# Softmax times V: the last head's scores in parts of 2, 2, 2, 1, 1 rows, with a store moved behind the first part

## Chip, cores, metric

The kernel runs on one core of a Trainium2 chip. The metric is the device time of that core in microseconds (us). A profile has its own zero, so moments of two profiles are compared with each other only to some tenths of a us, and where it matters against a landing of data in the same profile.

## The reference, cut to what matters

```
scores: 8 x 12 x 1024 x 1024, v: 8 x 12 x 1024 x 64, float32
attn = exp(scores - max);  attn = attn / (sum(attn) + 1e-8);  out = attn @ v
```

There are 96 heads of 4 MB of scores each, which are read once. The kernel leaves the maximum out and gets the sum from a column of ones beside V.

## The kernel before

Heads are worked on in groups of four; a loop runs over the 24 groups. A head is 128 partitions with 8 rows each. For each row ScalarE (ACT) makes the exponentials (two rows at a time), TensorE (PE) transposes them in 8 pieces into PSUM, VectorE (DVE) copies the transposed row to SBUF, and TensorE multiplies it with V in 8 matmuls of 65 columns. After four or eight rows VectorE divides by the sums. All loads and stores are issued by one engine (SP) into one queue.

```python
def finish(u):                        # the second product of one row
    ...
    for c in range(C):                # C = 8
        nc.tensor.matmul(
            out=bank[:, g * M : (g + 1) * M],          # M = 65
            lhsT=pt[:, c * P : (c + 1) * P],
            rhs=st["vones"][:, c, 0:M],
            start=(c == 0), stop=(c == C - 1),
        )
    ...
def load_next(k, n0):                 # heads 0 and 1 of the next group
    if k < AHEAD - 2:
        load(k, (n0 + (AHEAD + k)) % BH, cond=n0 < BH - AHEAD)

def last(n0):                         # at the end of a group
    with tc.If(n0 < BH - 2 * AHEAD) as cmp:            # the ordinary groups
        ...
    with cmp.Else():
        with tc.If(n0 < BH - AHEAD) as cmp2:           # the last group but one
            ...
            load(AHEAD - 2, BH - 2, (4, 4))            # the last head but one, in two parts
            load(AHEAD - 1, BH - 1, (4,))              # the last head: four rows,
            store(n0, AHEAD - T)                       # a store of two heads (512 KB),
            load(AHEAD - 1, BH - 1, (2, 1, 1), 4)      # and the other four rows
        ...
```

For each row TensorE issues, in its queue, the row's transposes, then the second product of an earlier row.

The softmax here doesn't subtract the row's maximum and nothing guards it: scores larger than these inputs give would overflow.

## Time and profile before

| | before |
|---|---|
| time, first three runs | 1066.0 us median (1065.59 to 1067.29) |
| busy: PE / DVE / ACT | 68% / 73% / 70% of the span |
| DMA | full in 39 of 40 slices, 434 GB/s |
| last row of scores landed, in the profile | 1052.8 us |
| VectorE's last multiply of the output by the reciprocal sums ended | 1059.4 us |
| span of the profile | 1063.5 us |

How to read it: the queue is full to the end, so the time is the bytes at the queue's rate, plus a tail of about 11 us behind the last bytes. Timeline: start, length, engine, line, operation; in brackets the idle time before and what ended it.

```profile
1049.29 0.69 DVE L285 COPY pt<-psT 128x1024 f16<-128x1024 f16 x1 [0.27 <-PE L146]
1050.25 0.69 DVE L285 COPY pt<-psT 128x1024 f16<-128x1024 f16 x1 [0.27 <-PE psO L146]
```

These are rows 0 and 1 of the last head. The copies start 0.96 us apart, though one takes 0.69, and each time a completion of TensorE ends 0.27 us of idle time. Row 1 had been ready in ScalarE long before.

### The profile page before, as it was taken

The page shows a single profiled execution, that of the slowest core. Times are in us where ns is not written, and L with a number is a line of the kernel's source. Part 1 is how long each engine was busy: PE and PEld are TensorE (multiplying, and loading weights), DVE is VectorE, ACT ScalarE, POOL GpSimd, SP SyncE. Part 2 cuts the span into 40 slices and gives each one's busy share as a digit, 9 for nine tenths or more (in the row PEclk, how much of TensorE's full clock was granted, in tenths as well). Part 3 has the DMA queues.
Part 4 walks back from the last instruction along what each step waited for, and adds up shares of the span by engine and source line. Part 5 has one row for each costly group of instructions (what it writes and reads, how often), then busy time and mean ns, then how long its engine had stood idle before and what let it go on. Part 6 is the DMA issues. An engine that isn't in the chain of part 4 may idle for free. (4 is left out here: it accounts for less than half of the span.)

```text
span 1063.5 us, 32373 instructions
## 1 busy us (share of the span) xinstructions
PE 725.8 (68%) x12288; PEld 669.1 (63%) x12288; DVE 780.7 (73%) x1589; ACT 743.2 (70%) x480; POOL 48.1 (5%) x31
## 2 busy tenths in 40 slices
PE   2487766667776767677676666767766767766676
PEld 2476666566666666566575666756666666666575
DVE  3488767777677776777777777777678776777777
ACT  3767776676766758676676766777766767667586
POOL 0000000000000000000000000000000000000000
PEclk9789888988879888988888888898889898888989
DMA  9999999999999999999999999999999999999995
GB/s 394 433 420 436 422 434 433 433 435 433 434 433 434 424 438 433 429 428 433 435 427 439 434 433 434 427 436 425 434 429 434 434 434 434 434 431 425 439 426 242
DMA packets 24915, 453.05 MB, mean 426 GB/s; under 512 B 2768, under 2 KB 2768, under 8 KB 9296
## 3 DMA queue, kind: packets, MB, share of 16 engines
q1 hardware_dynamic: 24912, 453.00, 99.2%
q8 instruction: 3, 0.05, 0.0%
HBM read 436.21 MB, written 25.17 MB: 434 GB/s over the span
## 5 line engine op out<-in xcount | busy, mean ns | idle before, releaser
L265 ACT ACTIVATE p_nat<-s_nat 128x2048 f16<-128x2048 f32 (+1 forms) x408 | 705.2, 1800 | 308.9 <-DMA s_nat<-in_scores_dram 218.0
L279 PE MATMUL psT<-order,p_nat 128*128 128x128 f16 x6144 | 556.7, 243 | 231.2 <-ACT p_nat L265 224.7
L285 DVE COPY pt<-psT 128x1024 f16<-128x1024 f16 x768 | 513.7, 687 | 221.8 <-PE L146 94.1
L279 PEld LDWEIGHTS <-p_nat 128*128 128x128 f16 x6144 | 437.8, 122 | 255.2 <-ACT p_nat L265 252.5
L146 PEld LDWEIGHTS <-pt 128*128 128x128 f16 x6144 | 296.9, 107 | 133.6 <-DVE pt L285 128.1
L146 PE MATMUL psO<-vones,pt 128*128 128x65 f16 x3072 | 183.6, 203 | 58.5 <-DVE pt L285 56.6
L146 PE MATMUL psO_whole<-vones,pt 128*128 128x65 f16 x3072 | 186.1, 209 | 42.6 <-DVE pt L285 42.6
L212 DVE COPY vones<-v_half 32x512 f16<-32x512 f16 x384 | 109.2, 284 | 28.3 <-POOL v_half L208 17.0
L208 POOL CAST v_half<-v_sb 128x2048 f16<-128x2048 f32 x25 | 47.4, 1894 | 995.4 <-DMA v_sb<-in_v_dram 915.9
L130 DVE TENSOR_TENSOR out_sb<-psO,recip 64x256 f32<-64x256 f32 x192 | 81.1, 423 | 6.1
L130 DVE TENSOR_TENSOR out_sb<-psO_whole,recip 64x512 f32<-64x512 f32 x96 | 66.1, 688 | 3.0
L258 ACT ACT_TABLE_LOAD x24 | 30.8, 1283 | 1.8 <-ACTq L309 1.4
L125 DVE RECIPROCAL recip<-psO 128x4 f32<-128x4 f32 x96 | 17.1, 179 | 18.4 <-PE psO L146 17.2
L258 ACT ACTIVATE spare<-order 128x1 f16<-128x1 f16 x48 | 9.5, 198 | 0.3
L125 DVE RECIPROCAL recip<-psO_whole 128x8 f32<-128x8 f32 x48 | 9.5, 197 | 0.0
L71 DVE MEMSET vones<- 128x16 f16 x4 | 0.2, 72 | 0.8 <-PEq L326 0.8
L62 DVE CAST order<-ident 128x128 f16<-128x128 f32 x1 | 0.2, 226 | 0.4 <-POOL ident masks.py:199 0.4
masks.py:199 POOL TENSOR_SCALAR_AFFINE_SELECT ident<-ident 128x128 f32<-128x128 f32 x1 | 0.3, 292 | 0.1
masks.py:197 POOL MEMSET ident<- 128x128 f32 x1 | 0.2, 204 | 0.3 <-POOLq L326 0.3
L326 POOL MEMSET const-float32-0.0<- 128x1 f32 x1 | 0.1, 98 | 0.2 <-issue 0.2
L326 POOL MEMSET const-bfloat16-1.0<- 128x1 bf16 x1 | 0.1, 101 | 0.0
L326 POOL MEMSET const-uint8-127<- 128x1 uint8 x1 | 0.1, 101 | 0.0
(1 smaller groups left out, 0.1 us busy)
## 6 DMA issues: line engine op xcount, KB each, us to landing
s_nat<-in_scores_dram SPq DMA_DIRECT2D x96, 4096.0 KB, 34.1
v_sb<-in_v_dram SPq DMA_DIRECT2D x24, 1024.0 KB, 35.7
out_dram<-out_sb SPq DMA_DIRECT2D x47, 512.0 KB, 25.3
s_nat<-in_scores_dram SPq DMA_DIRECT2D x3, 2048.0 KB, 32.7
s_nat<-in_scores_dram SPq DMA_DIRECT2D x1, 1024.0 KB, 25.6
s_nat<-in_scores_dram SPq DMA_DIRECT2D x2, 512.0 KB
out_dram<-out_sb SPq DMA_DIRECT2D x2, 256.0 KB, 2.1
```

The costliest lines, as they stand in the source:

```text
L62: nc.vector.tensor_copy(out=order16[:].rearrange("p (t j) -> p t j", t=T), in_=ident32[:].rearrange("p (j t) -> p t j", t=T),)
L71: nc.vector.memset(vo[:, :, D : D + 2], 1.0)
L125: nc.vector.reciprocal(out=recip, in_=psO[:, :, :, D : D + 1])
L130: nc.vector.tensor_tensor(out=rows.rearrange("j (b g) d -> j b g d", g=G), in0=psO[part, :, :, 0:D], in1=recip[part].to_broadcast([W, last ...
L146: nc.tensor.matmul(out=bank[:, g * M : (g + 1) * M], lhsT=pt[:, c * P : (c + 1) * P], rhs=st["vones"][:, c, 0:M], start=(c == 0), stop=(c ...
L208: nc.gpsimd.tensor_copy(out=v_half[:], in_=v_sb[:])
L212: copy = nc.vector.tensor_copy(out=vones_bufs[k][s * Q : (s + 1) * Q, :, 0:D].rearrange("i (h l) d -> i h l d", l=L), in_=v_half[k * Q : ( ...
L258: table = nc.scalar.activation(out=spare[:], in_=order16[:, 0:1], func=EXP)
L265: exp = nc.scalar.activation(out=p_nat[:, g : g + rows, :].rearrange("p r (x v) -> p x r v", v=Q * L), in_=s_bufs[k][:, r + g : r + g + ro ...
L279: nc.tensor.transpose(out=psT[:, c * P : (c + 1) * P], in_=p_row[:, c // L, c % L, :], identity=order16[:],)
L285: copy = nc.vector.tensor_copy(out=pt[:], in_=psT[:])
L326: nc = _bacc.Bacc("TRN2", target_bir_lowering=False, num_devices=1)
```

## The change

Its intent: ScalarE waits 1.02 us for the four-row part of the last head. With two rows first, and the store only then, it can go on at once.

```diff
                 load(AHEAD - 2, BH - 2, (4, 4))
-                load(AHEAD - 1, BH - 1, (4,))
+                load(AHEAD - 1, BH - 1, (2,))
                 store(n0, AHEAD - T)
-                load(AHEAD - 1, BH - 1, (2, 1, 1), 4)
+                load(AHEAD - 1, BH - 1, (2, 2, 1, 1), 2)
```

## The prediction

> **What bounds the kernel now.** I read the page's slices first, then the list of who waited for whom, then the timelines of the DMA queue's issuing engine (SP), ScalarE and VectorE over the last 60 us.
>
> ```profile
> DMA  9999999999999999999999999999999999999995
> GB/s 394 433 420 436 422 434 433 433 435 433 434 433 434 424 438 433 429 428 433 435 427 439 434 433 434 427 436 425 434 429 434 434 434 434 434 431 425 439 426 242
> ```
>
> The DMA engines are full in 39 of 40 slices, at about 434 GB/s; ACT (70%), DVE (73%) and PE (68%) have slack. So the length is the bytes over this rate (453 MB / 434 GB/s = 1044 us) plus what is left to compute after the last bytes. The changed code moves the same bytes, so only two things can move: whether the queue ever runs dry, and the tail behind the last loads. The tail starts from when each load was put in the queue; SP's timeline from 1005 us:
>
> ```profile
> 1006.69 0.36 SPq L166 DMA_DIRECT2D out_dram<-out_sb  x1
> 1007.68 6.48 SPq L189 DMA_DIRECT2D s_nat<-in_scores_dram  x3
> 1024.19 0.35 SPq L166 DMA_DIRECT2D out_dram<-out_sb  x1
> 1024.72 28.28 SPq L189 DMA_DIRECT2D s_nat<-in_scores_dram  x5
> 1053.29 6.71 SPq L166 DMA_DIRECT2D out_dram<-out_sb  x3
> ```
>
> The third load of the second line (issued 1013.83) is the last head's four-row part; the store at 1024.19 is the one behind it, then come two rows (1024.72), one row (1025.26), one row (1030.62). The last two L189 entries are the switched-off loads of the final iteration. Issue to landing, from the DMA view cut to one issue at a time: four rows 32.7 us, store 23.7, two rows 25.6. So they land at 1046.5, 1047.9 and 1050.3. For the two single rows the view has no landing, but the two switched-off loads wait on the same semaphores and went at 1051.70 and 1052.91, so they landed just before, about 1051.6 and 1052.8. The spacing is 1.2 us per 512 KB in the queue, whether load or store.
>
> ScalarE, where the last head begins:
>
> ```profile
> 1041.77 3.72 ACT L265 ACTIVATE p_nat<-s_nat 128x2048 f16<-128x2048 f32 x2 [0.19 <-PE L279]
> 1045.39 0.19 ACT L258 ACTIVATE spare<-order 128x1 f16<-128x1 f16 x1
> 1046.61 7.65 ACT L265 ACTIVATE p_nat<-s_nat 128x2048 f16<-128x2048 f32 x5 [1.02 <-DMA s_nat<-in_scores_dram]
> ```
>
> It is done with the head before at 1045.6, idles 1.02 us for the four-row part, and then runs its five exponentials (2, 2, 2, 1, 1 rows) without a gap over 0.1 us to 1054.26. Starts, from narrower windows: 1046.61, 1048.42, 1050.45, 1052.27, 1053.2. The third starts just after its landing at 1050.3: it is bound by data as much as by ScalarE.
>
> VectorE to the end:
>
> ```profile
> 1050.85 0.20 DVE L125 RECIPROCAL recip<-psO_whole 128x8 f32<-128x8 f32 x1
> 1051.27 0.69 DVE L285 COPY pt<-psT 128x1024 f16<-128x1024 f16 x1 [0.21 <-PE L279]
> 1051.99 1.41 DVE L130 TENSOR_TENSOR out_sb<-psO_whole,recip 64x512 f32<-64x512 f32 x2
> 1053.43 1.89 DVE L285 COPY pt<-psT 128x1024 f16<-128x1024 f16 x3
> 1055.23 0.17 DVE L125 RECIPROCAL recip<-psO 128x4 f32<-128x4 f32 x1
> 1055.32 0.66 DVE L285 COPY pt<-psT 128x1024 f16<-128x1024 f16 x1
> 1056.01 0.88 DVE L130 TENSOR_TENSOR out_sb<-psO,recip 64x256 f32<-64x256 f32 x2
> 1056.92 0.69 DVE L285 COPY pt<-psT 128x1024 f16<-128x1024 f16 x1
> 1058.33 0.18 DVE L125 RECIPROCAL recip<-psO 128x4 f32<-128x4 f32 x1 [0.72 <-PE psO L146]
> 1058.55 0.87 DVE L130 TENSOR_TENSOR out_sb<-psO,recip 64x256 f32<-64x256 f32 x2
> ```
>
> This carries the end. From the copy at 1051.27 VectorE is never idle until the last copy ends at 1057.61. In program order that first copy is row 2 of the last head (third of eight), then come the normalisation of the head before (1.41), the copies of rows 3, 4, 5, a reciprocal, row 6, half a normalisation, and row 7. The last copy is not waiting for ScalarE, which ended at 1054.26: it stands in VectorE's own line, and the line's start is set by row 2. Row 2 hangs on the second exponential (1048.42 to 1050.33), its transposes (from 1050.38) and the copy at 1051.27.
>
> **What the Trainium skill says.** "DMA: Bandwidth & Descriptors", section "Queues, rings and completion order": descriptors are consumed in ring order on each DMA engine. The trace agrees: the landings above come in the order of issue, at the queue's rate. The section "Why a DMA increments its semaphore by 16 and not by 1" says that only the full count of 16 means that all data landed, so a part is usable when its slowest engine is through; the DMA share falls well under full from 1049 on while rows still land to 1052.8, which agrees. The section "Anatomy of one DMA — SWDGE (gpsimd) path" has a fixed 2.0 us per DMA (for the GpSimd path), and says that DMA engines do not wait on semaphores, the issuing sequencer does. In this full queue the fixed part does not show (1.2 us for a whole 512 KB part); it shows on the last, lone stores of 256 KB (2.1 us). So a fifth part is nearly free.
>
> **The change part by part.** (1) First part two rows instead of four: 1 MB less in front of the store. From the spacing, 2 x 1.2 = 2.4 us: rows 0 and 1 land at 1046.5 - 2.4 = 1044.1, before ScalarE is free at 1045.6. The first exponential starts at about 1045.6, which takes away the whole wait of 1.02. (2) The store follows: 1044.1 + 1.4 = 1045.5 (the store's own step was 1047.9 - 1046.5). (3) The new two-row part, rows 2 and 3, is now behind the store: 1045.5 + 2.4 = 1047.9. Adding the 0.1 us seen from landing to start (1046.5 to 1046.61), the second exponential starts at 1048.03 where it was 1048.42: 0.39 sooner, with a new wait of about 0.6 for DMA in front of it. (4) Rows 4 and 5, 6, 7 have the same bytes ahead of them as before: 1050.3, 1051.6, 1052.8. Exponentials three to five start as before, ScalarE ends at 1054.2 as before. (5) One more DMA in the kernel: its completion on a full queue, I take 0.0 to 0.05 us.
>
> On VectorE: row 2's copy moves from 1051.27 to 1050.88. The line behind it (1.41 + three copies at 0.6 + 0.1 + 0.66 + 0.88 + 0.69) moves as a block if no member waits. Row 4: its exponential ends at 1052.36, transposes take 0.64, ready about 1053.1; its new place is 1053.65. Row 5 follows at 1054.25, ready about 1053.7. Row 6: exponential ends 1053.31, transposed about 1054.0, place 1054.9. Row 7: exponential ends 1054.26, transposed by about 1055.3, place 1056.5. None is short, so the block keeps the 0.39 us. The last stores go 0.39 sooner. Sum of the tail: -0.39 + 0.03 = about -0.4 us.
>
> (6) The hidden part. The instruction order shows that the DMA semaphores, eight, are used in rotation, and that branches of unequal DMA count are evened out by register steps and waits. The extra DMA makes SP in the ordinary branch (the iterations before the last two) wait also for the landing of the store of heads 0 and 1, before the next iteration's first load. Before, it already waits there for the load of head 1:
>
> ```profile
> SPq L231 <- SPq L231: 134.2, 21, 7.1
> ```
>
> In the iteration at 979 that wait ended at 986.8, and the next load was issued at 988.19. The store follows head 1's load in the queue, so its landing is 1.2 to 1.4 us later, and the load would be issued at about 989.6. But that load's data is used at 1020.98, 32.8 us after issue, while its own 4.19 MB need 4.19 / 434 = 9.7 us. So some 23 us of transfers stand ahead of it, and 1.4 us less of lead costs nothing. The next load waits for ScalarE (issued 994.31), and isn't touched. In the last-but-one iteration the last row's load must now wait for that store's landing, about 1032, twenty microseconds before its turn. No cost.
>
> Total: 1066.0 - 0.4 = 1065.6 us.
>
> **The rivals.** All of ScalarE's 1.02 us comes off the end: 1065.0. For it speaks that this is the only wait for data in the tail, and the intent is plainly this; against it that rows 2 and 3 are put behind the store, and rows 4 to 7 land no sooner. Nothing comes off: 1066.0; so it is if ScalarE's last three exponentials, whose data do not move, set the end. Against it is VectorE's unbroken line of 6.3 us that starts at row 2. The wait for the store in (6) starves the queue: at 1.4 us in 22 iterations it would be +31 us, 1097, slower by 2.9%; the 23 us of lead speak against it. A short dip from smaller parts (8 KB a row of partition instead of 16) would cost under 0.5 us: the two-row part before the change kept the pace of 1.2 per 512 KB.
>
> **Range and chances.** The effect is under 0.1%, less than the spread of the three runs before (1065.59 to 1067.29). The range is that spread around 1065.6, a bit widened for another chip: 1064.2 to 1067.0. Faster by over 2% would need 21 us, and the tail behind the last data is only about 11 us long: 0.003. Slower needs the starved queue: 0.007. The same: 0.99.
>
> **What would show it.** The first exponential of the last head at about 1045.6 with no wait; a new wait of about 0.6 for DMA before the second; the third to fifth at the same places; VectorE's block and its last multiply about 0.4 sooner; SP's wait at L231 longer by about 1.3 us in each iteration, with DMA still full in 39 slices. I am wrong if VectorE's line breaks at row 4 (then the gain is 0 to 0.2), if the part behind the store lands later than 1048, or if the slices show DMA under 9 before the last.

## The result

| | before | changed |
|---|---|---|
| times | 1065.8 us median of 4 (1065.54 to 1067.29) | 1066.18 us median of 4 (1065.52 to 1066.19) |
| ratio | | 0.9999, 95% interval 0.9982 to 1.0017: the same |
| span of the profile | 1063.5 | 1063.6 |

A ratio here is the mean time of one kernel's fast runs over that of the other's of the same rounds, so not quite the ratio of the medians.

The slices of the changed kernel: DMA is full up to the last, as before.

```profile
DMA  9999999999999999999999999999999999999995
```

ScalarE at the last head, in the changed kernel:

```profile
1045.29 1.90 ACT L265 ACTIVATE p_nat<-s_nat 128x2048 f16<-128x2048 f32 x1
1047.88 1.92 ACT L265 ACTIVATE p_nat<-s_nat 128x2048 f16<-128x2048 f32 x1 [0.70 <-PE psT L279]
1050.30 3.81 ACT L265 ACTIVATE p_nat<-s_nat 128x2048 f16<-128x2048 f32 x3 [0.50 <-PE psO L146]
```

The wait of 1.02 is gone. A wait of 0.70 stands before the second exponential instead, and one of 0.50 before the third. The profile names PE as what ended them; but rows 2 and 3 landed at 1047.8 (issue at 1023.22 plus 24.6 us) and the exponential started 0.1 later, so it was the load. The second exponential is 0.54 us sooner than before (1048.42), the later ones 0.15, which is as much as the data landed sooner in this profile.

VectorE to the end, in the changed kernel:

```profile
1049.38 0.69 DVE L285 COPY pt<-psT 128x1024 f16<-128x1024 f16 x1 [0.27 <-PE psT L279]
1050.34 0.69 DVE L285 COPY pt<-psT 128x1024 f16<-128x1024 f16 x1 [0.27 <-PE L279]
...
1051.36 0.69 DVE L285 COPY pt<-psT 128x1024 f16<-128x1024 f16 x1 [0.21 <-PE L146]
1052.08 1.41 DVE L130 TENSOR_TENSOR out_sb<-psO_whole,recip 64x512 f32<-64x512 f32 x2
...
1058.64 0.88 DVE L130 TENSOR_TENSOR out_sb<-psO,recip 64x256 f32<-64x256 f32 x2
```

Nothing moved forward here: the copies and the last multiply are 0.09 us *later* than before. The data came sooner, the exponentials came sooner, and VectorE did not notice. The copies of rows 0 and 1 are again 0.96 us apart with 0.27 of idle time each.

Last, SP's own wait where the groups' branches meet; the columns are us in all, times, longest:

```profile
SPq L231 <- SPq L231: 161.4, 43, 7.2
```

It was 134.2 before: (161.4 - 134.2) / 22 = 1.24 us more in each ordinary iteration, for the landing of the store. The queue stayed full, so it cost nothing.

### The profile page after: what moved, and what is told of

Its sections match the earlier page's. It is cut to its first block, busy times and chain, and to the rows that moved or that the text cites. A ratio compares the mean times of both kernels' runs of the same rounds, so it can differ in the third digit from the quotient of the medians.

```text
span 1063.6 us, 32424 instructions
## 1 busy us (share of the span) xinstructions
PE 724.6 (68%) x12288; PEld 667.7 (63%) x12288; DVE 780.9 (73%) x1589; ACT 743.3 (70%) x480; POOL 48.0 (5%) x31
```

## The theory and its rivals

A semaphore is a counter by which one engine tells another how far it is. In the trace, every weight load and every matmul of TensorE adds one to one semaphore, 12288 of each. Of the steps between these additions in the kernel before, 22647 of 24578 are 30 ns; the two shortest are 29 ns. An extract of their times from the kernel before:

```
1050.013  1050.043  1050.073  1050.103  1050.133  1050.163  1050.193 ...
333 additions from 1046.9 to 1056.9 us; the kernel's only pause over 0.1 us
between 1043 and 1056.9 is one of 0.11 us at 1046.75
```

A row has 16 weight loads and 16 matmuls, so 32 x 30 ns = 0.96 us, exactly the spacing of the copies. TensorE itself is faster: earlier in the kernel before, at full clock, the transposes of successive rows start at 1028.35, 1029.05 and 1029.75, 0.70 us apart.

```profile
1028.35 0.61 PE L279 MATMUL psT<-order,p_nat 128*128 128x128 f16 x8
1029.05 0.61 PE L279 MATMUL psT<-order,p_nat 128*128 128x128 f16 x8
```

So TensorE's work gets ahead of its own count, and VectorE, which waits for the count, learns of a row late. Read from the traces (the ends of matmuls are modelled by the profile):

| last head | last transpose ended | its addition came | VectorE's copy started |
|---|---|---|---|
| before, row 1 | 1049.91 | 1050.22 | 1050.25 |
| before, row 2 | 1051.02 | 1051.24 | 1051.27 |
| changed, row 1 | 1049.52 | 1050.32 | 1050.34 |
| changed, row 2 | 1050.85 | 1051.34 | 1051.36 |

Each copy follows its addition by 0.02 to 0.03 us, and the addition follows the work by up to 0.80 us. In the changed kernel the transposes of row 2 also began late, at 1050.21: in TensorE's queue they stand behind a matmul that waits for VectorE's copy of row 0 (1049.38 to 1050.07), and that copy had itself waited for the count.

*Theory of the count:* the count, not the data, sets when row 2's copy starts, so the change has nothing to gain. *Rivals:* (a) the prediction's own, in which row 2's exponential sets it; (b) the landings of the last head; (c) the time of TensorE itself, in its array or in loading weights; (d) VectorE's own work; (e) TensorE's granted clock, which from 1034 to 1038 us was 0.60 in the changed kernel's profile and 1.00 in that of the kernel before.

Ten more kernels were run, two of them twice. The quantities to compare, all read from the traces: the *lag* is from the end of the second exponential (rows 2 and 3) to row 2's copy; the *tail* is from the landing of the last row to the end of VectorE's last multiply; the clock is TensorE's mean granted clock from 1034 to 1038 us. (One of them, split_fine, ended so much later that it does not stand in the table.)

| kernel | counts per row, last head | row 2's exponential ends | row 2's copy | lag | tail | clock | span |
|---|---|---|---|---|---|---|---|
| before | 32 | 1050.33 | 1051.27 | 0.94 | 6.64 | 1.00 | 1063.5 |
| changed | 32 | 1049.80 | 1051.36 | 1.56 | 6.87 | 0.60 | 1063.6 |
| cut_only | 32 | 1048.84 | 1051.73 | 2.89 | 7.42 | 0.74 | 1064.0 |
| narrow_after | 32 | 1050.41 | 1051.69 | 1.29 | 6.58 | 1.00 | 1063.9 |
| more_after | 48 | 1050.34 | 1052.25 | 1.91 | 10.19 | 1.00 | 1067.5 |
| half_before | 24 | 1049.96 | 1050.72 | 0.76 | 6.29 | 1.00 | 1062.9 |
| half_before2 | 24 | 1049.98 | 1050.74 | 0.76 | 6.29 | 1.00 | 1062.8 |
| half_after | 24 | 1049.12 | 1049.88 | 0.76 | 5.85 | 1.00 | 1062.1 |
| half_after2 | 24 | 1049.22 | 1050.53 | 1.31 | 6.42 | 0.80 | 1062.6 |
| half_cut | 24 | 1048.46 | 1049.74 | 1.29 | 5.69 | 1.00 | 1061.8 |
| split_before | 32 | 1051.93 | 1052.87 | 0.94 | 6.62 | 1.00 | 1065.0 |
| split_after | 32 | 1051.51 | 1052.27 | 0.76 | 6.27 | 1.00 | 1064.6 |
| split_late | 32 | 1050.49 | 1052.72 | 2.24 | 6.76 | 1.00 | 1065.1 |

## The experiments

### cut_only: the cut without the store's move

```diff
-                load(AHEAD - 1, BH - 1, (4,))
+                load(AHEAD - 1, BH - 1, (2, 2))
                 store(n0, AHEAD - T)
```

> The kernel before with the last head in 2,2,2,1,1 rows, but the store left where it was, behind row 3 (one half of the change alone). Theory of the count: TensorE's completions reach VectorE through one semaphore that rises once per weight load and once per matmul, 30 ns apart in both traces, 32 per row = 0.96 us per row, without a pause from about 1043 to 1057; the end hangs on this count and not on the last head's data, so the profiled span stays at 1063.5 +- 0.3 (VectorE's last copy at 1056.9 to 1057.1 if the count starts as in the two kernels). Theory of the prediction (VectorE's line starts at row 2, and row 2 at its exponential): the second exponential starts at about 1047.1 without a wait, 1.3 us sooner than before, so the span falls by 0.4 to 1.0 us, to 1062.5 to 1063.1. The time moves by less than 0.1% in both.

Measured: 1066.12 us (1065.76 to 1066.66) against 1065.98, ratio 1.0004 (0.9987 to 1.0020). ScalarE and VectorE at the last head:

```profile
1045.14 3.70 ACT L265 ACTIVATE p_nat<-s_nat 128x2048 f16<-128x2048 f32 x2
1050.12 3.81 ACT L265 ACTIVATE p_nat<-s_nat 128x2048 f16<-128x2048 f32 x3 [1.28 <-PE psO_whole L146]
```
```profile
1049.75 0.69 DVE L285 COPY pt<-psT 128x1024 f16<-128x1024 f16 x1 [0.27 <-PE psT L279]
1050.71 0.69 DVE L285 COPY pt<-psT 128x1024 f16<-128x1024 f16 x1 [0.27 <-PE L279]
1051.73 0.69 DVE L285 COPY pt<-psT 128x1024 f16<-128x1024 f16 x1 [0.21 <-PE L146]
```

Here the first four rows' exponentials run without a wait, and row 2 is ready at 1048.84, a microsecond and a half sooner than before. Its copy starts at 1051.73, no sooner: 2.89 us behind. The copies of rows 0 and 1 keep their 0.96. Rival (a) is out for this profile, and so is (b) for rows 0 to 3. The span of 1064.0 is 0.2 above what the count's theory allowed, and the last copy, at 1057.38, 0.3 later. The likely reason is in the table's clock column: TensorE was granted 0.74 of its clock from 1034 to 1038, and steps of 76 to 77 ns stand in the count from 1032.9 to 1035.6. So this run alone does not answer rival (e); the next one does.

### narrow_after and more_after: fewer columns, more counts

```diff
 narrow_after (changed kernel; wrong results on purpose)
+        w0 = 0 if k < 2 else M - 8
-                out=bank[:, g * M : (g + 1) * M],    rhs=st["vones"][:, c, 0:M],
+                out=bank[:, g * M + w0 : (g + 1) * M],  rhs=st["vones"][:, c, w0:M],

 more_after (changed kernel; right results)
+        cuts = (0, M) if k < AHEAD - 1 else (0, 33, M)
+        for lo, hi in zip(cuts, cuts[1:]):   # the loop over c goes inside
-                out=bank[:, g * M : (g + 1) * M],    rhs=st["vones"][:, c, 0:M],
+                out=bank[:, g * M + lo : g * M + hi],   rhs=st["vones"][:, c, lo:hi],
```

> The changed kernel with the second product of heads 2 and 3 cut to the last 8 of its 65 columns (wrong results on purpose): as many weight loads and matmuls, an eighth of the columns streamed. Theory of the count: nothing changes, span within 0.3 us of the changed kernel (1063.6). Theory of TensorE's array time: the second product's part of a row, 8 matmuls some 33 ns apart, gets shorter, by 0.1 us or more per row over 16 rows, so the end comes 1 us or more sooner.

> The changed kernel with the second product of the last head of each group in 33 and 32 columns, each with its own eight weight loads (right results; same columns in all): 48 counts per row of that head instead of 32. Theory of the count: 0.48 us more for each of its rows; six rows' worth stand before row 7's transposes and two behind, so from the last row's landing to VectorE's last multiply it is 9.7 to 10.8 us instead of 6.9 (changed kernel), the span 3 to 4 us longer. Theory of VectorE's line or of the landings: below 0.5 us, as VectorE's work and the loads are the same.

Measured: narrow_after 1066.42 us (1066.0 to 1066.9), ratio 1.0006 (0.9990 to 1.0023): an eighth of the columns in the second product of two heads of four, and nothing is gained in time. The second product's matmuls started 25 ns apart instead of 33, 0.06 us less per row, so some 1.0 us over the 16 rows was to be had if the array set the pace; that speaks against the array's time in rival (c). This run also answers rival (e): it has the changed loads, 32 counts per row, and the full clock. Measured back from the landing of the last row, its second exponential ended 0.37 us sooner than in the kernel before, as predicted for the change, but row 2's copy started only 0.03 us sooner, and the tail is 6.58 against 6.64. The changed kernel's own tail of 6.87 is longer by 0.3, which may be its slower clock. more_after 1069.33 us (1068.78 to 1070.58), ratio 1.0034 (1.0020 to 1.0048); its tail is 10.19 us, in the range told ahead of it. VectorE's copies of rows 5 and 6 of the last head in it:

```profile
1056.51 0.69 DVE L287 COPY pt<-psT 128x1024 f16<-128x1024 f16 x1 [0.75 <-PE L148]
...
1057.95 0.69 DVE L287 COPY pt<-psT 128x1024 f16<-128x1024 f16 x1
```

They start 1057.95 - 1056.51 = 1.44 us apart, which is 48 x 30 ns. VectorE's work and the loads are those of the changed kernel, so rivals (b) and (d) do not give these three microseconds. Weight loads were never varied apart from the count, so that they set the pace (the rest of rival (c)) is not excluded by the totals. The trace speaks against it: row 5's last transpose had ended at 1054.83 and was counted at 1056.49, 1.66 us later, with up to 59 finished instructions not yet counted.

### half_before, half_after and half_cut: fewer counts

```diff
 (wrong results on purpose; on the kernel before, the changed kernel, and cut_only)
+        wide = 1 if k < 2 else 2
-        for c in range(C):
+        for c in range(0, C, wide):
-                out=bank[:, g * M : (g + 1) * M],
+                out=bank[:, g * M : (g + wide) * M].rearrange("p (a m) -> p a m", a=wide),
-                rhs=st["vones"][:, c, 0:M],
+                rhs=st["vones"][:, c : c + wide, 0:M],
```

> The kernel before with the second product of heads 2 and 3 of each group in 4 matmuls of 130 columns instead of 8 of 65 (wrong results on purpose; same columns streamed, half the instructions and half the weight loads): 24 counts per row instead of 32. Theory of the count: 24 x 30 ns = 0.72 us per row, below ScalarE's 0.9, so TensorE no longer lags at the end, the end hangs on the landing of the last row (1052.8) plus its own chain, and the span falls by 1.0 to 2.1 us, to about 1061.5 to 1062.5. Theory of TensorE's array time: the columns are the same, so the span moves by less than 0.5. Theory of VectorE's line: VectorE does the same work, so its block stays 6.3 us long and moves only with row 2; less than 0.5.

> The changed kernel with the same halving of the second product's instructions for heads 2 and 3 (wrong results on purpose). Theory of the count: once the count no longer binds, the change can pay: span 0 to 0.5 us under half_before, and 1.0 to 2.5 under the changed kernel. Theory of the prediction: 0.4 under half_before too, but half_before then equals the kernel before. If neither halved kernel falls by 0.5 us the theory of the count is out.

> half_before once more, for the difference to half_after: from the last row's landing to the last multiply 6.3 +- 0.15 us.

> half_after once more: from the last row's landing to the last multiply 5.85 +- 0.15 us, 0.3 to 0.6 less than half_before2; times of the two apart by 0.04%, less than five rounds can tell.

> Halved instructions of the second product for heads 2 and 3 (wrong results on purpose) with the cut alone, 2,2,2,1,1 rows and the store behind row 3. Theory of the count: with the count relieved row 2's copy follows its exponential by about 0.75 us, as in both halved kernels, unless VectorE is still at rows 0 and 1; from the last landing to the last multiply 5.5 to 5.9 us (half_after 5.84, half_before 6.29). If the place of the store mattered by itself, it would be 0.5 under half_after or more.

Times in two batches, each against the kernel before of its own rounds:

| | first batch (before: 1065.98) | second batch (before: 1065.82) |
|---|---|---|
| half_before | 1064.74, ratio 0.9990 (0.9973 to 1.0006) | 1064.69, ratio 0.9989 (0.9975 to 1.0003) |
| half_after | 1064.77, ratio 0.9990 (0.9974 to 1.0007) | 1064.25, ratio 0.9985 (0.9972 to 0.9999) |
| half_cut | | 1064.28, ratio 0.9984 (0.9970 to 0.9998) |

VectorE at the last head, first in half_before, then in half_after:

```profile
1048.92 1.41 DVE L286 COPY pt<-psT 128x1024 f16<-128x1024 f16 x2 [0.27 <-PE psO_whole L147]
...
1050.72 0.69 DVE L286 COPY pt<-psT 128x1024 f16<-128x1024 f16 x1 [0.28 <-PE L280]
```
```profile
1045.10 4.28 DVE L286 COPY pt<-psT 128x1024 f16<-128x1024 f16 x7
...
1049.88 0.69 DVE L286 COPY pt<-psT 128x1024 f16<-128x1024 f16 x1 [0.38 <-PE L280]
```

Three things follow. First, the waits of 0.27 between rows 0 and 1 are gone, and in half_after seven copies run without a gap. Second, where TensorE had its full clock, row 2's copy follows its exponential by 0.76 us in both kernels: this is the lag when the count is not late. So here rival (a), the prediction's mechanism, does hold, and the change pays what it should: the tail is 5.85 us against 6.29. Third, half_before fell by 0.6 us of span, where 1.0 or more was expected: from row 2's copy to the end VectorE still has its block of 7.9 us, so a relieved count could bring only the start of it forward. half_after's span is 0.8 us under half_before's, where 0 to 0.5 was expected; 0.4 of it is that the last row landed sooner in that profile.

half_before2 met its expectation (6.29). half_after2 missed it (6.42, not 5.85). TensorE's clock differed. The columns of this view are the stretch, then busy time of PE, PEld, DVE, ACT and POOL, and at the end the granted clock, the DMA share and GB/s; first half_after, then half_after2:

```profile
1030.00:1034.00 4.00, 3.06 (x65) 2.81 (x63) 3.12 (x6) 4.00 (x3) 0.00 (x0) 1.00 1.03 441
1034.00:1038.00 4.00, 3.34 (x65) 2.82 (x63) 3.72 (x8) 4.00 (x3) 0.00 (x0) 1.00 1.01 434
```
```profile
1030.00:1034.00 4.00, 2.10 (x28) 2.11 (x29) 1.71 (x4) 4.00 (x3) 0.00 (x0) 0.78 1.03 440
1034.00:1038.00 4.00, 3.71 (x67) 3.55 (x64) 3.33 (x7) 4.00 (x3) 0.00 (x0) 0.80 0.97 418
```

Part of the 65 matmuls belong to the head before, so the counts are the fairer comparison: from 1032 to 1036 TensorE's count rose by 131 in half_after and by 102 in half_after2, which had 17 steps of 76 or 77 ns there. VectorE was still busy with the backlog, copy after copy at 0.60 us, when row 2 came. So the gain of 0.44 us is there in one pair of profiles and hidden in the other, and the times of these kernels cannot tell them apart. half_cut, with rows 2 and 3 not behind the store, has a tail of 5.69, as told ahead: in these profiles the place of the store was worth 0.15 us. Its lag is 1.29, as row 2's transposes stood behind a matmul that waited for row 0's copy (1048.22 to 1048.91).

### split_before, split_after, split_late, split_fine: why the count is late, and an attempt to use it

A likely reason for the late count: the third head from the end lands whole at 1030.5, after which 24 rows x 0.96 = 23.0 us must pass, while the last row lands 22.2 us later. Loading that head in halves gives TensorE a start.

```diff
 split_before, split_after (on the kernel before and the changed kernel)
-            load(k, (n0 + (AHEAD + k)) % BH, cond=n0 < BH - AHEAD)
+            parts = (R,) if k == 0 else (R // 2, R // 2)
+            load(k, (n0 + (AHEAD + k)) % BH, parts, cond=n0 < BH - AHEAD)

 split_late: split_after with the store behind row 5
+                load(AHEAD - 1, BH - 1, (2, 2, 2));  store(...);  load(AHEAD - 1, BH - 1, (1, 1), 6)

 split_fine: split_after with the last head but one in 2, 2, 4 rows
+                load(AHEAD - 2, BH - 2, (2, 2, 4))
```

> The kernel before, with head 1 of each group (so also the third head from the end) loaded in two halves instead of whole. Theory of the count: TensorE's count falls behind because the third head from the end lands whole at 1030.5; until then the count stands still for 1.1 us, and 24 rows x 0.96 = 23.0 us from there run past the last landing (1052.8). With the head in halves the count goes on at 1031.6 without a pause, but then reaches the last head at about 1047.3 and waits there for its four-row part (exponential done at 1048.5): the end comes 0.4 to 1.0 us sooner than before. Rival (landings of the last head alone set the end): nothing changes, within 0.3.

> The changed kernel with the same halves. Theory of the count: the count is no longer late when the last head begins, so here the two-row first part (exponential done at 1047.2 or before) pays: the end comes 1.0 to 2.0 us sooner than in the changed kernel and 0.4 to 1.3 sooner than in split_before. Rival (the first part's size never mattered, whatever the count): equal to split_before within 0.2.

> The halves, the last head in 2,2,2,1,1 rows, and the store behind row 5 instead of row 1, so that rows 2 to 5 land 1.2 us sooner and rows 6 and 7 as before. Theory of the count with halves: at most 0.5 us sooner than split_after, if the rows in the middle then hold the count up; the normalisation of the head before needs the store landed (about 1050.3 against 1051), so no loss. Theory that nothing but the last row's landing counts now: equal to split_after within 0.2.

> The halves, the changed last head, and the second head from the end in 2,2,4 rows instead of 4,4. Theory of the count: ScalarE reaches this head at about 1035.7, and its four-row part lands at 1036.8, so up to 1.1 us of pause goes: 0 to 0.6 us sooner than split_after if the count still trails at the end, nothing if it has caught up by then.

| | time, us | ratio to before (1066.22) |
|---|---|---|
| split_before | 1067.61 (1066.95 to 1068.13) | 1.0013 (1.0000 to 1.0027) |
| split_after | 1066.40 (1066.33 to 1067.14) | 1.0003 (0.9989 to 1.0017) |
| split_late | 1066.81 (1066.11 to 1066.99) | 1.0003 (0.9989 to 1.0017) |
| split_fine | 1081.15 (1080.67 to 1081.66) | 1.0138 (1.0122 to 1.0153) |

Row 0's copy of the last head in split_before, and then the copies of rows 0 and 2 in split_after:

```profile
1050.89 0.69 DVE L286 COPY pt<-psT 128x1024 f16<-128x1024 f16 x1 [0.91 <-PE L146]
```
```profile
1050.20 0.69 DVE L286 COPY pt<-psT 128x1024 f16<-128x1024 f16 x1 [0.27 <-PE psT L280]
...
1052.27 0.69 DVE L286 COPY pt<-psT 128x1024 f16<-128x1024 f16 x1 [0.30 <-PE L146]
```

With the head in halves the count is no longer late when split_before reaches the last head, and its four-row part makes it wait: 0.91 us before row 0's copy, and a pause of 0.57 us in the count at 1049.74. In split_after this is gone. Its count is still late at rows 0 and 1 (row 1 ended at 1050.34 and was counted at 1051.14), has caught up at row 2, where the lag is 0.76, and the tail is 0.35 us shorter (6.27 against 6.62). In this pair the times differ too: the slowest run of split_after (1067.14) is 0.47 us under the median of split_before, though not under its fastest (1066.95), and the means are 1066.60 and 1067.60. The tail accounts for a third of this difference of 1.0; the rest is not explained.

But both expectations of a gain over the unsplit kernels missed. One DMA more per group, on a queue that is always full, is not free. From the fourth group to the fourteenth, the landings of the groups' first heads fall behind those of the kernel before by 0.42 to 0.43 us in each of the four split kernels, 0.04 us per group and DMA; in the unsplit kernels the same difference is 0.04 us at most. Over the 22 groups ahead of the last group's scores this is an estimated 0.9 us, more than the split gives. (The last group's first head landed 1.6 us later in split_before, 1022.5 against 1020.9, but only 0.4 later in split_fine; this late in the kernel the unsplit profiles too differ by up to 1.2 us.) So no version with right results was found that beats both kernels.

split_late cannot be judged by its profile: TensorE's granted clock was 0.63 in 1046 to 1050, against 1.00 in split_after. Its time is not told apart from split_after's.

split_fine missed its expectation by far; its loss of 15 us has another cause. ScalarE before the last head but one, in split_fine:

```profile
1053.14 7.32 ACT L266 ACTIVATE p_nat<-s_nat 128x2048 f16<-128x2048 f32 x4 [15.70 <-DMA s_nat<-in_scores_dram]
```

That head's first two rows had landed at 1034.65; the exponential started 0.1 us after the very last row of the *last* head, at 1053.04. DMAs take eight semaphores in turn; in this branch there are now nine loads and stores from this part to row 7, and the trace shows that the first and the last of them report to the same semaphore (115). That the exponential's wait asks for the value after both is argued from this and these two times; no run took the sharing away by itself.

## Why the prediction was right or wrong

The number was right: 1065.6 us predicted, 1066.18 measured, inside the range. For the effect itself this was luck: the range is 2.8 us wide, the forecast effect 0.4, and "no change" would have been as right. Point by point:

* *What bounds the kernel* was right: full slices, and no change in them.
* *Steps 1 to 3, the loads,* were right to 0.2 us. Rows 0 and 1 landed at 1043.9 (1044.1 predicted), the store at 1045.4 (1045.5), rows 2 and 3 at 1047.8 (1047.9). The first exponential lost its wait and started at 1045.29 (1045.6); the second one got a new wait, 0.70 us against 0.6.
* *Step 4* was right: rows 4 to 7 landed, and their exponentials ran, where they had been, all about 0.15 us sooner in this profile. *Step 5* (0.0 to 0.05 us for one more DMA) fits the 0.04 us of the split kernels.
* *"On VectorE: row 2's copy moves from 1051.27 to 1050.88"* is the step that failed. It rests on "Row 2 hangs on the second exponential". That exponential ended 0.53 us sooner and the copy started 0.09 later. The runs showed the count of TensorE's completions in its place: 30 ns for each of 32 instructions per row. In the kernel before the two limits were nearly even: the lag was 0.94, and 0.76 is the lag when the count is not late. So the count already bound row 2, 0.18 us behind the limit that the data set, and from earlier data nothing was to be had. Where the count was relieved, the predicted 0.4 appeared in two pairs of profiles (half_after 0.44, split_after 0.35) and was hidden by a slower clock in a third (half_after2).
* *VectorE's block to the end* was right: from row 2's copy to the last multiply it is 8.15 us in both kernels. One reading in it was off: row 6 was "transposed about 1054.0", and in the trace its last transpose ended at 1054.67, as it stands behind a second product that waits for row 3's copy. It moves with the block, so the sum does not change.
* *Step 6, the hidden wait,* was right: 1.24 us more per iteration, 1.2 to 1.4 predicted, and no cost.
* Of *the rivals*, "nothing comes off" is the one that came true, but for another reason than the one given for it. ScalarE's last exponentials do not set the end in the kernels as they are, since relieving the count moves it.

An effect of 0.04% could not have been seen in these times in either case; the failed step shows only in the profile.

## What to carry to other kernels

When an engine waits a short, even time before every step, and the engine it waits for is done by then, look at the spacing of the steps: 0.96 us per row was the number of TensorE's instructions times the 30 ns at which their completions are counted, and neither earlier data nor fewer columns moved it. Before taking a wait away, look for a second limit and work out which of the two binds; here the wait was 1.02 us, and the second limit already lay 0.18 us beyond what the data allowed. A further part of the last load cost nothing that could be measured here (changed, cut_only); in a loop on a full queue each one cost 0.04 us.

## What the Trainium skill lacked or had wrong

* "TensorE: Matmul & The Clock Gate", section "The cost: per-tile semaphore tail", says that completions that each increment a semaphore serialize; its fit for the tail has 26.3 ns per increment and 4.7 ns per tile, 31.0 for a tile with its own increment. This would have pointed to the failed step, had the prediction used it. The runs agree with the sum, not with 26.3 alone: 30 ns (0.96 and 1.44 us per row for 32 and 48 increments). They also show what the section does not say: weight loads count as matmuls do, and it is not only a tail behind one group of matmuls. It set the pace of a stage for 10 us.
* "DMA: Bandwidth & Descriptors", section "Anatomy of one DMA — SWDGE (gpsimd) path", has a fixed cost of 2.0 us per DMA, for the GpSimd path. On the full queue of SP here one more DMA cost 0.04 us (0.42 to 0.43 us over ten of them).
* "DMA: Bandwidth & Descriptors", section "Why a DMA increments its semaphore by 16 and not by 1", treats two DMAs in flight that share a semaphore, but only for a wait that passes too early. That the earlier one's consumer can be held until the later one lands, it does not say; split_fine lost 15.7 us in a wait that fits this.
